# Backward log-softmax on one core: y in pieces of 5120 and 11264 columns, the first piece ahead of each store, and hand-made synchronization

## The chip, the cores and the metric

The kernel runs on one core of a Trainium2 chip. Times are device microseconds (us) of that core. A few words used below: VectorE (DVE in the profile), ScalarE (ACT) and SyncE (SP; its DMA issues are SPq) are engines of the core. A transfer is issued by SyncE into a queue that 16 DMA engines work off; every transfer here is split over all 16. A "packet" is one row of a transfer as the trace records it, with its start, duration and size. The profile's span runs from the first to the last instruction; a launch takes about 1.8 us more than its span (1867.19 against 1865.4 us in the profiled run of the kernel before).

## The reference

```python
# y, dy: (8, 1024, 8192) float32
def reference(y, dy):
    softmax_x = np.exp(y)
    sum_dy = np.sum(dy, axis=-1, keepdims=True)
    return dy - softmax_x * sum_dy
```

Each of 8192 rows is independent. The work is to read y and dy once and to write the result once: 805 MB.

## The kernel before

The rows go through in 32 groups of 256: 128 partitions with R = 2 rows each, so a group is 128 x 16384 numbers (8.4 MB) of each array. dy is loaded whole and the result overwrites it. y comes in two loads of 8192 columns. There are two buffers for dy and one for each half of y. The Tile framework places all waits.

```python
    R = 2
    CD = D // 2
    # dyp: 2 buffers of [P, R * D]; yp: R buffers of [P, D]          (cut)

    def load_dy(g):
        dy_t = dyp.tile([P, R * D], fp32, name="dy_t")
        nc.sync.dma_start(out=dy_t[:], in_=dy_v[g])
        s_t = stats.tile([P, R], fp32, name="s_t")
        nc.vector.tensor_reduce(out=s_t[:], in_=..., op=ALU.add, negate=True)   # (cut)
        return dy_t, s_t

    def load_y(g):
        y_ts = []
        for r in range(R):
            y_t = yp.tile([P, D], fp32, name="y_t")
            nc.sync.dma_start(out=y_t[:], in_=y_v[g][:, r * D : (r + 1) * D])
            y_ts.append(y_t)
        return y_ts

    def compute(dy_t, s_t, y_ts):
        for r in range(R):
            for c in range(0, D, CD):
                e = y_ts[r][:, c : c + CD]
                d = dy_t[:, r * D + c : r * D + c + CD]
                nc.scalar.activation(e, e, EXP)
                nc.vector.scalar_tensor_tensor(
                    out=d, in0=e, scalar=s_t[:, r : r + 1], in1=d, op0=ALU.mult, op1=ALU.add
                )
    # ...
    cur = load_dy(0)
    for g in range(G):
        if g < G - 1:
            y_ts = load_y(g)
            compute(*cur, y_ts)
            nxt = load_dy(g + 1)
            if g < G - 2:
                store(g, cur[0])
                cur = nxt
            # ... (the last store is cut in two)
```

In steady state SyncE issues: store of group g, both y loads of g+1, and, when that store has landed, dy of g+2.

## Time and profile before

| | kernel before |
|---|---|
| time, median of the 6 runs taken with those of the changed kernel | 1867.28 us |
| span of the profiled run | 1865.4 us |
| VectorE / ScalarE busy | 60% / 25% |
| DMA queue q1, share of 16 engines | 99.9% |
| rate over the span | 432 GB/s |

The first view is the page of the kernel before. The digits are busy tenths in 40 equal slices of the span; part 3 gives the time of the packets as a share of 16 engines; part 4 is the chain of waits, followed back from the last instruction; in part 5 the numbers after the bar are busy us, mean ns of one, and idle us before it with what ended it.

```profile
span 1865.4 us, 712 instructions
DVE 1119.2 (60%) x160; ACT 457.1 (25%) x129; POOL 0.2 (0%) x4
...
DMA  9999999999999999999999999999999999999999
...
q1 hardware_dynamic: 18576, 805.31, 99.9%
HBM read 536.87 MB, written 268.44 MB: 432 GB/s over the span
...
DMA y_t<-in_y_dram 69%; DVE dy_t L70 15%; ACT y_t L69 6%; DMA dy_t<-in_dy_dram 3%; DVE s_t L47 2%; DMA out_dram<-dy_t 1%; SPq L60 1%; SPq L77 1%; DVEq L122 0%; ACTq L69 0%; DVEq L70 0%
...
L69 ACT ACTIVATE y_t<-y_t 128x4096 f32<-128x4096 f32 x128 | 455.9, 3608 | 1375.6 <-DMA y_t<-in_y_dram 1375.6
```

Two readings of this page compete. By the chain, nearly one us in four is VectorE or ScalarE work (15 + 6 + 2%), so less of it, or earlier, should help. By the DMA row, the transfers never stop, and the engines' work lies behind them. The timeline decides how near the queue comes to running dry. Here are SyncE's issues in two late groups (start us, duration, instruction, count), and the VectorE sum that starts when dy is seen to have landed.

```profile
1709.76 0.33 SPq L45 DMA_DIRECT2D dy_t<-in_dy_dram  x1
...
1741.77 0.34 SPq L77 DMA_DIRECT2D out_dram<-dy_t  x1
1742.21 0.85 SPq L60 DMA_DIRECT2D y_t<-in_y_dram  x2
1748.49 17.22 DVE L47 TENSOR_REDUCE s_t<-dy_t 128x2 f32<-128x16384 f32 x1 [6.75 <-DMA dy_t<-in_dy_dram]
1767.83 0.33 SPq L45 DMA_DIRECT2D dy_t<-in_dy_dram  x1
```

The store is issued at 1741.77, and dy, the last transfer ahead of it in the queue, is seen to have landed at 1748.49. I call these 6.7 us the lead of the store. As long as the lead is large enough, the 16 engines pass from one transfer to the next without a stop. The dy load of 1767.83 has two y loads ahead of it.

### The profile page before, as it was taken

What the parts mean: (1) busy time and instruction counts of PE and PEld (TensorE: products, weight loads), DVE (VectorE), ACT (ScalarE), POOL (GpSimd) and SP (SyncE); (2) the same over time, 40 slices, a digit from 0 to 9 for tenths busy, and PEclk for the clock granted to TensorE, in tenths of its full rate; (3) what the DMA queues carried; (4) which work ended last, traced back from release to release, by engine and by line L of the source; (5) the groups of instructions that cost most, each with busy time, mean ns of one, the idle gap of its engine ahead of it and who ended that gap; (6) DMA issues with size and microseconds to landing.
All of it is one profiled execution on the core that took longest, in us unless ns stands there. A gap on an engine that the chain in (4) does not pass through costs nothing.

```text
span 1865.4 us, 712 instructions
## 1 busy us (share of the span) xinstructions
DVE 1119.2 (60%) x160; ACT 457.1 (25%) x129; POOL 0.2 (0%) x4
## 2 busy tenths in 40 slices
DVE  5675555755557555575555755657656576565664
ACT  2123321233212332123321233212332113331132
POOL 0000000000000000000000000000000000000000
DMA  9999999999999999999999999999999999999999
GB/s 427 416 434 431 443 433 422 435 437 436 427 433 431 440 430 434 431 429 441 433 437 425 433 442 431 434 425 436 438 434 433 428 434 437 437 431 430 429 435 396
DMA packets 18582, 805.36 MB, mean 432 GB/s; under 512 B 2064, under 2 KB 2064, under 8 KB 2064
## 3 DMA queue, kind: packets, MB, share of 16 engines
q1 hardware_dynamic: 18576, 805.31, 99.9%
q14 instruction: 6, 0.05, 0.0%
HBM read 536.87 MB, written 268.44 MB: 432 GB/s over the span
## 4 chain that ended last, share of the span: by engine, by line
DMA 74%; DVE 17%; ACT 6%; SPq 1%; issue 1%; DVEq 0%; ACTq 0%
DMA y_t<-in_y_dram 69%; DVE dy_t L70 15%; ACT y_t L69 6%; DMA dy_t<-in_dy_dram 3%; DVE s_t L47 2%; DMA out_dram<-dy_t 1%; SPq L60 1%; SPq L77 1%; DVEq L122 0%; ACTq L69 0%; DVEq L70 0%
## 5 line engine op out<-in xcount | busy, mean ns | idle before, releaser
L70 DVE SCALAR_TENSOR_TENSOR dy_t<-y_t,s_t,dy_t 128x4096 f32<-128x4096 f32 x128 | 568.1, 4481 | 490.3 <-ACT y_t L69 490.1
L69 ACT ACTIVATE y_t<-y_t 128x4096 f32<-128x4096 f32 x128 | 455.9, 3608 | 1375.6 <-DMA y_t<-in_y_dram 1375.6
L47 DVE TENSOR_REDUCE s_t<-dy_t 128x2 f32<-128x16384 f32 x32 | 551.0, 17220 | 232.1 <-DMA dy_t<-in_dy_dram 232.1
L69 ACT ACT_TABLE_LOAD x1 | 1.3, 1283 | 0.7 <-PEq L111 0.7
L111 POOL MEMSET const-bfloat16-1.0<- 128x1 bf16 x1 | 0.1, 102 | 0.0
L111 POOL MEMSET const-uint8-127<- 128x1 uint8 x1 | 0.1, 102 | 0.0
L111 POOL MEMSET const-float32-1.0<- 128x1 f32 x1 | 0.1, 99 | 0.0
L111 POOL MEMSET const-float32-0.0<- 128x1 f32 x1 | 0.1, 98 | 0.2 <-issue 0.2
## 6 DMA issues: line engine op xcount, KB each, us to landing
y_t<-in_y_dram SPq DMA_DIRECT2D x64, 4096.0 KB, 35.9
out_dram<-dy_t SPq DMA_DIRECT2D x2, 4096.0 KB, 22.6
dy_t<-in_dy_dram SPq DMA_DIRECT2D x32, 38.7
out_dram<-dy_t SPq DMA_DIRECT2D x31, 26.1
```

The lines of the kernel that those rows point to most:

```text
L47: nc.vector.tensor_reduce(out=s_t[:], in_=dy_t[:].rearrange("p (r d) -> p r d", r=R), axis=mybir.AxisListType.X, op=ALU.add, negate=True,)
L60: nc.sync.dma_start(out=y_t[:], in_=y_v[g][:, r * D : (r + 1) * D])
L69: nc.scalar.activation(e, e, EXP)
L70: nc.vector.scalar_tensor_tensor(out=d, in0=e, scalar=s_t[:, r : r + 1], in1=d, op0=ALU.mult, op1=ALU.add)
L77: nc.sync.dma_start(out=out_v[g][:, k * w : (k + 1) * w], in_=dy_t[:, k * w : (k + 1) * w])
L111: nc = _bacc.Bacc("TRN2", target_bir_lowering=False, num_devices=1)
```

## The change

Its intent is to make the lead larger and better balanced. y of a group is cut into 5120 and 11264 columns. The first piece needs only a part of the buffer that the group before has done with early, so it can be queued ahead of the store, after dy. While VectorE finishes the group, dy and that piece keep the queue filled. The dy load that waits for the store to land has the second piece, 11264 columns, ahead of it. The work on the second piece is cut so that its first multiply-add starts early (1024, 2048, 2048, 3072, 3072 columns). All engines are synchronized by hand in one critical section, with every wait written out, and the first dy load is cut in two.

```diff
+    A = 5120
+    PIECES = [(0, A), (A, 6144), (6144, 8192), (8192, 10240), (10240, 13312), (13312, W)]   # lines joined
+    x_ts = [pool.tile([P, W], fp32, name=f"x{j}") for j in range(2)]
+    y_t = pool.tile([P, W], fp32, name="y_t")
+    with tc.tile_critical(no_gpsimd_drain=True):
+        # ... semaphores, one per purpose
+        def load_ya(g):
+            if g:
+                nc.sync.wait_ge(dve_done, K * (g - 1) + 1)
+            nc.sync.dma_start(out=y_t[:, :A], in_=y_v[g][:, :A]).then_inc(ya_in, 16)
+        def load_yb(g):
+            if g:
+                nc.sync.wait_ge(dve_done, K * g)
+            nc.sync.dma_start(out=y_t[:, A:], in_=y_v[g][:, A:]).then_inc(yb_in, 16)
+        # ... first dy in two halves, load_ya(0)
+        for g in range(G - 1):
+            load_yb(g)
+            if g >= 1:
+                nc.sync.wait_ge(out_done[(g + 1) % 2], 16 * ((g + 1) // 2))
+            j = (g + 1) % 2
+            nc.sync.dma_start(out=x_ts[j][:], in_=dy_v[g + 1]).then_inc(dy_in[j], 16)
+            load_ya(g + 1)
+            if g == G - 2:
+                load_yb(g + 1)
+            else:
+                nc.sync.wait_ge(dve_done, K * (g + 1))
+            nc.sync.dma_start(out=out_v[g], in_=x_ts[g % 2][:]).then_inc(out_done[g % 2], 16)
+        # ... last store in two halves, waits for all stores; loops of ScalarE and VectorE over PIECES
-    cur = load_dy(0)
-    for g in range(G):
-        if g < G - 1:
-            y_ts = load_y(g)
-            compute(*cur, y_ts)
-            nxt = load_dy(g + 1)
-            if g < G - 2:
-                store(g, cur[0])
-        # ...
```

More of the change, by code (lines that the diff above doesn't have):

```diff
@@ L30 @@
     R = 2
+    W = R * D
     G = N // (P * R)
-    assert N == G * P * R
-    CD = D // 2
+    assert N == G * P * R and D == 8192 and G >= 3
+    A = 5120
+    PIECES = [
+        (0, A),
+        (A, 6144),
+        (6144, 8192),
+        (8192, 10240),
+        (10240, 13312),
+        (13312, W),
+    ]
+    K = len(PIECES)
+    ROW0 = 3
     y_v = y.flatten_outer_dims().rearrange("(g p r) d -> g p (r d)", p=P, r=R)
@@ L37 @@
     out_v = out.flatten_outer_dims().rearrange("(g p r) d -> g p (r d)", p=P, r=R)
-    dyp = ctx.enter_context(tc.tile_pool(name="dyp", bufs=2))
-    yp = ctx.enter_context(tc.tile_pool(name="yp", bufs=R))
-    stats = ctx.enter_context(tc.tile_pool(name="stats", bufs=2))
-    def load_dy(g):
-        dy_t = dyp.tile([P, R * D], fp32, name="dy_t")
-        nc.sync.dma_start(out=dy_t[:], in_=dy_v[g])
-        s_t = stats.tile([P, R], fp32, name="s_t")
-        nc.vector.tensor_reduce(
-            out=s_t[:],
-            in_=dy_t[:].rearrange("p (r d) -> p r d", r=R),
-            axis=mybir.AxisListType.X,
-            op=ALU.add,
-            negate=True,
-        )
-        return dy_t, s_t
@@ L56, in load_y @@
-    def load_y(g):
-        y_ts = []
-        for r in range(R):
-            y_t = yp.tile([P, D], fp32, name="y_t")
-            nc.sync.dma_start(out=y_t[:], in_=y_v[g][:, r * D : (r + 1) * D])
-            y_ts.append(y_t)
-        return y_ts
-    def compute(dy_t, s_t, y_ts):
-        for r in range(R):
-            for c in range(0, D, CD):
-                e = y_ts[r][:, c : c + CD]
-                d = dy_t[:, r * D + c : r * D + c + CD]
-                nc.scalar.activation(e, e, EXP)
-                nc.vector.scalar_tensor_tensor(
-                    out=d, in0=e, scalar=s_t[:, r : r + 1], in1=d, op0=ALU.mult, op1=ALU.add
-                )
@@ L74, in store @@
-    def store(g, dy_t, parts=1):
-        w = R * D // parts
-        for k in range(parts):
-            nc.sync.dma_start(
-                out=out_v[g][:, k * w : (k + 1) * w], in_=dy_t[:, k * w : (k + 1) * w]
-            )
-    cur = load_dy(0)
-    for g in range(G):
-        if g < G - 1:
-            y_ts = load_y(g)
-            compute(*cur, y_ts)
-            nxt = load_dy(g + 1)
-            if g < G - 2:
-                store(g, cur[0])
-                cur = nxt
-            else:
-                held, cur = cur, nxt
-        else:
-            y_ts = load_y(g)
-            compute(*cur, y_ts)
-            store(g - 1, held[0])
-            store(g, cur[0], parts=R)
+    pool = ctx.enter_context(tc.tile_pool(name="pool", bufs=1))
@@ new lines @@
+    x_ts = [pool.tile([P, W], fp32, name=f"x{j}") for j in range(2)]
+    y_t = pool.tile([P, W], fp32, name="y_t")
+    s_ts = [pool.tile([P, R], fp32, name=f"s{j}") for j in range(2)]
+    with tc.tile_critical(no_gpsimd_drain=True):
+        dy_in = [nc.alloc_semaphore(f"dy_in{j}") for j in range(2)]
+        dy_in_row = nc.alloc_semaphore("dy_in_row")
+        ya_in = nc.alloc_semaphore("ya_in")
+        yb_in = nc.alloc_semaphore("yb_in")
+        out_done = [nc.alloc_semaphore(f"out_done{j}") for j in range(2)]
+        row_done = nc.alloc_semaphore("row_done")
+        exp_done = nc.alloc_semaphore("exp_done")
+        sum_done = nc.alloc_semaphore("sum_done")
+        dve_done = nc.alloc_semaphore("dve_done")
+        def load_ya(g):
[6 more added lines that the diff above has]
+            nc.sync.dma_start(out=y_t[:, A:], in_=y_v[g][:, A:]).then_inc(yb_in, 16)
+        nc.sync.dma_start(out=x_ts[0][:, :D], in_=dy_v[0][:, :D]).then_inc(dy_in_row, 16)
+        nc.sync.dma_start(out=x_ts[0][:, D:], in_=dy_v[0][:, D:]).then_inc(dy_in[0], 16)
+        load_ya(0)
+        for g in range(G - 1):
[10 more added lines that the diff above has]
+            nc.sync.dma_start(out=out_v[g], in_=x_ts[g % 2][:]).then_inc(out_done[g % 2], 16)
+        last = x_ts[(G - 1) % 2]
+        nc.sync.wait_ge(dve_done, K * (G - 1) + ROW0)
+        nc.sync.dma_start(out=out_v[G - 1][:, :D], in_=last[:, :D]).then_inc(row_done, 16)
+        nc.sync.wait_ge(dve_done, K * G)
+        nc.sync.dma_start(out=out_v[G - 1][:, D:], in_=last[:, D:]).then_inc(
+            out_done[(G - 1) % 2], 16
+        )
+        nc.sync.wait_ge(out_done[(G - 2) % 2], 16 * (G // 2))
+        nc.sync.wait_ge(row_done, 16)
+        nc.sync.wait_ge(out_done[(G - 1) % 2], 16 * (G // 2))
+        for g in range(G):
+            for k, (b, e) in enumerate(PIECES):
+                if k == 0:
+                    nc.scalar.wait_ge(ya_in, 16 * (g + 1))
+                elif k == 1:
+                    nc.scalar.wait_ge(yb_in, 16 * (g + 1))
+                nc.scalar.activation(y_t[:, b:e], y_t[:, b:e], EXP).then_inc(exp_done, 1)
+        for g in range(G):
+            x, s = x_ts[g % 2], s_ts[g % 2]
+            for c, w, sem, v in (
+                [(0, D, dy_in_row, 16), (D, D, dy_in[0], 16)]
+                if g == 0
+                else [(0, W, dy_in[g % 2], 16 * (g // 2 + 1))]
+            ):
+                nc.vector.wait_ge(sem, v)
+                nc.vector.tensor_reduce(
+                    out=s[:, c // D : (c + w) // D],
+                    in_=x[:, c : c + w].rearrange("p (r d) -> p r d", d=D),
+                    axis=mybir.AxisListType.X,
+                    op=ALU.add,
+                    negate=True,
+                ).then_inc(sum_done, 1)
+            nc.vector.wait_ge(sum_done, g + 2)
+            for k, (b, e) in enumerate(PIECES):
+                r = b // D
+                nc.vector.wait_ge(exp_done, K * g + k + 1)
+                nc.vector.scalar_tensor_tensor(
+                    out=x[:, b:e],
+                    in0=y_t[:, b:e],
+                    scalar=s[:, r : r + 1],
+                    in1=x[:, b:e],
+                    op0=ALU.mult,
+                    op1=ALU.add,
+                ).then_inc(dve_done, 1)
```

## The prediction

> **What bounds the kernel now.** The transfers, and nothing else. The page's DMA row is 9 in all 40 slices, queue q1 is busy 99.9% of the 16 engines' span, and 805.31 MB move at a mean of 432 GB/s. VectorE is busy 60% and ScalarE 25%. In the DMA records of the trace the typical 64 KB packet takes 2.418 us and the typical 32 KB packet 1.213 us, which is 433.7 and 432.2 GB/s over 16 engines. The Trainium skill ("DMA: Bandwidth & Descriptors", section "Where 436 GB/s comes from") puts the ceiling of the fabric at 435.2 GB/s; this trace agrees, it runs 0.4% under it while packets flow. Engine by engine I find six gaps of 0.3 us in the whole run.
>
> The chain of waits looks different: 69% of it is the wait for y, 15% VectorE, 6% ScalarE. I read that as a queue that is always full: a y load takes 44.5 us from issue to landing although its 4 MB need about 9.7 us, so it stands behind other transfers. The steady period of a group is 58.08 us (chain view, 1452.30 to 1510.38), and one group's packets per engine are 16 x 2.418 + 16 x 1.213 = 58.1 us. So the period holds no bubble.
>
> **Why the queue never empties before.** In the timeline a store is issued at 1741.77; the load of dy ahead of it is seen landed at 1748.49, so the store is 6.7 us early. The next dy load is issued at 1767.83, when the store has landed, with the two y loads (19.4 us of packets) still queued.
>
> **What the change does.** The bytes are the same. The issues go from 129 to 130, with pieces of 20 and 44 KB a partition instead of twice 32 KB. From the two packet times a packet costs about 8 ns plus 0.0368 ns per byte (estimate), so 20 + 44 KB cost 2.43 us, as 2 x 1.213 do: nothing. The queue order becomes dy(g+1), first y piece, store(g), rest of y. Estimates from 4096-column durations (ScalarE 3.56 us, VectorE 4.44 us): after the rest of y lands, the five pieces end about 14 us later, while dy plus the first piece keep the queue filled for 25 us, so the store is some 11 us early instead of 7. The next dy load waits for the store with 13.3 us of y behind it: again 11 us spare. A margin over zero buys no time. Splitting the first dy is off the path too. Hand-made waits add short instructions, inside slack.
>
> **What lies on the critical path.** The head (first packet 1.7 us after the start), the packets (about 1859 us), and the tail (last packet to end 1.2 us). Packets that run over their typical time sum to about 4 us an engine. Only head, tail and this excess can move, by a microsecond or so.
>
> **Predicted:** 1867.4 us, 8 in 10 between 1865.6 and 1869.4. Chances: faster by over 2% 0.01, within 2% 0.98, slower 0.01.
>
> **Right if** the DMA row stays at 9, q1 at about 99.9%, the rate at 432 GB/s, the period at 58.1 us; the waits of the engines and the chain's labels change much; and the store's issue leads the landing of the transfers ahead of it by about 11 us.
>
> **Wrong if** 20 KB packets or the new order of reads and writes run at another rate (period not 58.1 us at full queue: the packet times would show it), if some wait holds SyncE longer than the queued work lasts (DMA slices under 9), or if the hand synchronization adds microseconds at the start or end of the kernel (first packet later than 1.7 us, last packet to end over 1.2 us).

## The result

| | before | changed |
|---|---|---|
| median of 6 runs, us | 1867.28 | 1869.47 |
| lowest to highest, us | 1866.88 to 1867.93 | 1868.34 to 1869.74 |
| span of the profiled run, us | 1865.4 | 1867.7 |

The ratio is 1.001, with a 95% interval of 0.9997 to 1.0023: the same at the 2% mark. The changed kernel is 2 us slower, 0.1%, and in these runs the two ranges don't overlap.

The page of the changed kernel, the lines that answer to those shown of before:

```profile
span 1867.7 us, 633 instructions
DVE 1130.5 (61%) x225; ACT 463.3 (25%) x193; POOL 0.2 (0%) x4
...
DMA  9999999999999999999999999999999999999998
...
q1 hardware_dynamic: 18720, 805.31, 99.8%
HBM read 536.87 MB, written 268.44 MB: 431 GB/s over the span
...
DMA y_t<-in_y_dram 70%; DVE x L136 19%; ACT y_t L114 5%; DMA x<-in_dy_dram 2%; DMA out_dram<-x 2%; DVE s L125 1%; SPq L95 1%; SPq L73 0%; SPq L82 0%; SPq L81 0%; SPq L169 0%; SPq L58 0%
...
L114 ACT ACTIVATE y_t<-y_t 128x5120 f32<-128x5120 f32 (+2 forms) x192 | 462.0, 2469 | 1373.6 <-DMA y_t<-in_y_dram 1373.6
```

ScalarE's wait for y is as long as it was (1373.6 against 1375.6 us), and the queue is as full. Its timeline at the same place:

```profile
1745.14 0.34 SPq L95 DMA_DIRECT2D out_dram<-x  x1
1745.53 0.43 SPq L78 DMA_DIRECT2D y_t<-in_y_dram  x1
1750.30 17.22 DVE L125 TENSOR_REDUCE s<-x 128x2 f32<-128x16384 f32 x1 [5.19 <-DMA x<-in_dy_dram]
1756.38 4.47 ACT L114 ACTIVATE y_t<-y_t 128x5120 f32<-128x5120 f32 x1 [15.46 <-DMA y_t<-in_y_dram]
1767.56 5.55 DVE L136 SCALAR_TENSOR_TENSOR x<-y_t,s,x 128x5120 f32<-128x5120 f32 x1
1775.72 0.33 SPq L89 DMA_DIRECT2D x<-in_dy_dram  x1
...
1789.01 9.97 ACT L114 ACTIVATE y_t<-y_t 128x1024 f32<-128x1024 f32 x5 [28.16 <-DMA y_t<-in_y_dram]
```

The store goes out at 1745.14, and the transfer ahead of it is now the first piece of y, which lands at 1756.38: a lead of 11.2 us in place of 6.7. The dy load of 1775.72 leads the landing of the second piece at 1789.01 by 13.3 us, where that of the kernel before (1767.83) led the landing of the second y load (1787.27) by 19.4. So 6.7 and 19.4 us have become 11.2 and 13.3, larger where it was small and better balanced. The intent was met. The steady group shows what it brought. The view is of one group's period, its length, busy us of VectorE, ScalarE and GpSimd, clock, DMA share and GB/s, first in the kernel before.

```profile
1452.30:1510.38 58.08, 34.98 (x5) 14.25 (x4) 0.00 (x0) 1.00 1.00 433
```

The same view of the changed kernel:

```profile
1455.25:1513.31 58.06, 35.33 (x7) 14.44 (x6) 0.00 (x0) 1.00 1.00 433
```

The period is the time that the packets need, in both, at 433 GB/s.

To place the 2 us, I cut each span into the head (up to the first packet of data), the stretch of packets, and the tail (after the last packet), from the packet records:

```
                 span     head   packets  tail
before          1865.42   1.74   1862.46  1.22
before_again    1864.71   1.73   1861.76  1.21
before_hand     1866.08   1.94   1862.47  1.67
after           1867.65   1.96   1864.05  1.64
after_again     1866.79   1.95   1863.20  1.64
after_even      1867.03   1.96   1863.41  1.66
```

(The runs other than "before" and "after" are described below.) The head is 0.2 us and the tail 0.4 us longer in the changed kernel. The other 1.6 us arise between the packets of the first ten groups: the last sum of the steady part starts 1.8 us later than before, and it did so 1.9 us later by the tenth group already.

### The profile page after: what moved, and what is told of

The parts are those of the page before. It is cut to its first block, busy times and chain, and to the rows that moved or that the text cites. A ratio compares the mean times of both kernels' runs of the same rounds, so it can differ in the third digit from the quotient of the medians. Undisturbed runs are those within 1.5% of the kernel's fastest.

```text
span 1867.7 us, 633 instructions
## 1 busy us (share of the span) xinstructions
DVE 1130.5 (61%) x225; ACT 463.3 (25%) x193; POOL 0.2 (0%) x4
## 4 chain that ended last, share of the span: by engine, by line
DMA 73%; DVE 20%; ACT 5%; SPq 1%; issue 0%
DMA y_t<-in_y_dram 70%; DVE x L136 19%; ACT y_t L114 5%; DMA x<-in_dy_dram 2%; DMA out_dram<-x 2%; DVE s L125 1%; SPq L95 1%; SPq L73 0%; SPq L82 0%; SPq L81 0%; SPq L169 0%; SPq L58 0%
## 5 line engine op out<-in xcount | busy, mean ns | idle before, releaser
L136 DVE SCALAR_TENSOR_TENSOR x<-y_t,s,x 128x5120 f32<-128x5120 f32 (+2 forms) x192 | 579.3, 3059 | 538.3 <-ACT y_t L114 537.2
L114 ACT ACTIVATE y_t<-y_t 128x5120 f32<-128x5120 f32 (+2 forms) x192 | 462.0, 2469 | 1373.6 <-DMA y_t<-in_y_dram 1373.6
L125 DVE TENSOR_REDUCE s<-x 128x2 f32<-128x16384 f32 (+1 forms) x33 | 551.2, 16703 | 174.8 <-DMA x<-in_dy_dram 174.8
```

Of the source, the lines that this page charges most:

```text
L114: nc.scalar.activation(y_t[:, b:e], y_t[:, b:e], EXP).then_inc(exp_done, 1)
L125: nc.vector.tensor_reduce(out=s[:, c // D : (c + w) // D], in_=x[:, c : c + w].rearrange("p (r d) -> p r d", d=D), axis=mybir.AxisListType ...
L136: nc.vector.scalar_tensor_tensor(out=x[:, b:e], in0=y_t[:, b:e], scalar=s[:, r : r + 1], in1=x[:, b:e], op0=ALU.mult, op1=ALU.add,).then_i ...
```

## The experiments

The theory: the queue of transfers is the bound, in both kernels, and a lead beyond what keeps it full buys nothing. The rivals: the chain is right that the engines' work is part of the path; or something was gained in the steady part and lost elsewhere.

### 1. Nearly no compute: after_tiny

```diff
-nc.scalar.activation(y_t[:, b:e], y_t[:, b:e], EXP)
+nc.scalar.activation(y_t[:, b:b + 64], y_t[:, b:b + 64], EXP)
 # likewise 64 columns in each sum and in each multiply-add
```

> The changed kernel with every exp, sum and multiply-add cut to 64 columns of its piece; all transfers and waits stay (the result is wrong on purpose). Theory (the transfers are the bound, the engines only wait for them): 1867 to 1870 us, no faster than the kernel before, within 0.2% of it; VectorE and ScalarE under 3% busy. Rival (the chain of waits is right that VectorE and ScalarE make up 20 to 25% of the path): 1400 to 1500 us.

Measured: 1869.64 us (4 runs), ratio 1.0009. The page of this run:

```profile
span 1867.0 us, 633 instructions
DVE 52.6 (3%) x225; ACT 36.3 (2%) x193; POOL 0.2 (0%) x4
...
DMA  9999999999999999999999999999999999999998
...
q1 hardware_dynamic: 18720, 805.31, 99.9%
```

VectorE's work fell from 1130.5 to 52.6 us, and the time did not move. The quarter of the chain that was put down to VectorE and ScalarE was not worth one us. The chain is true as a story of who released whom, but each y load that it counts had stood in a full queue, and a y load that is issued later stands there for a shorter time.

A remark on the side: the comparison with the reference let this kernel pass, although it computes a wrong result. A softmax over 8192 columns averages 1/8192. If dy is drawn with a spread of 1, a sum of 8192 draws has a size of about 90, so the term is about 0.01 beside a dy of about 1. Here a passed comparison is weak evidence that a kernel is right.

### 2. The same added work in both kernels: plus4, plus9, plus17

If the lead is what the change altered, it must show when each group gets more work ahead of its store. The added work is a sum over columns of y that nothing uses, before the last multiply-add; the result stays right.

```diff
# kernel before, in compute(), after the activation
+                if r == R - 1 and c == D - CD:
+                    j_t = junk.tile([P, 1], fp32, name="j_t")
+                    nc.vector.tensor_reduce(out=j_t[:], in_=y_ts[r][:], axis=..., op=ALU.add)
# changed kernel, VectorE loop, after the wait for the exp
+                if k == K - 1:
+                    nc.vector.tensor_reduce(out=junk[:, g : g + 1], in_=y_t[:, A : A + D], axis=..., op=ALU.add)
# plus4: 4096 of the columns; plus17: the sum of 8192 twice
```

> The kernel before with one added sum of 8192 columns of y (about 8.6 us on VectorE) in each group, ahead of the last multiply-add, so each store is issued some 8.6 us later. Theory (the store leads the end of the dy packets by some 5 us, so 8.6 us overrun the lead by about 3 us in each of 31 groups): 1950 us, 1920 to 1980, the DMA queue no longer full (q1 about 95%). Rival (VectorE has 40% idle time, so 8.6 us of it cost nothing): 1867 us.

> The changed kernel with the same added sum of 8192 columns (about 8.6 us) ahead of the last multiply-add of each group. Theory (the first piece of y ahead of the store makes the lead about 10 us, more than 8.6): 1869 to 1873 us, q1 still over 99.5%. Rival (both kernels have the same slack): the same loss as the kernel before with the same added work, some 80 us.

> The kernel before with one added sum of 4096 columns (about 4.4 us) in each group, so a store is issued only some 2.3 us before the landing of dy is seen, as it was 2.6 us before the landing of the first piece of y in the changed kernel with 8.7 us added. Theory (what counts is the lead of the store, whatever the kernel): a loss of the same kind, about 0.8 us a group, 1885 to 1905 us in all. Rival (the changed kernel's loss with 8.7 us added was its own, from its pieces or waits): 1867 us.

> The changed kernel with the same 4.4 us added in each group; its store should still lead by some 6.9 us, as that of the kernel before does with nothing added. Theory: 1868 to 1870 us, no loss against the changed kernel. Rival: the loss of before_plus4.

> The kernel before with two added sums of 8192 columns (17.3 us in a group). With 8.68 us added it lost 4.38 us a group, so once the lead is used up every added us should be a us of the period: 58.07 + 4.38 + 8.6 = 71.0 us a group, 2260 to 2280 us.

> The changed kernel with the same 17.3 us added. Its store's lead was 11.2 us against 6.75 us, so it should lose 4.5 us a group less than the kernel before with the same work: 66.6 us a group, 2120 to 2145 us. If the lead is no longer what counts, 71 us as the other.

| added per group (trace) | kernel before | changed kernel |
|---|---|---|
| nothing | 1867.28 us | 1869.47 us |
| 4.41 us (plus4) | 1892.00, ratio 1.0122 (1.0107 to 1.0137) | 1869.57, ratio 1.0005 (0.9989 to 1.0022) |
| 8.68 us (plus9) | 2000.26, ratio 1.0709 (1.0693 to 1.0725) | 1882.55, ratio 1.0071 (1.0054 to 1.0089) |
| 17.27 us (plus17) | 1981.30 (2 runs; not the same order, see below) | 2137.39 (2 runs) |

All ratios are against the unaltered kernel before. With 4.41 us added, the kernel before loses 1.2% and the changed one nothing; with 8.68 us it is 7.1% against 0.7%. This is what the change is worth, and it is not a matter of time saved. The expectations held for the plus4 runs and for after_plus17. after_plus9 missed its 1869 to 1873 us (four runs, 1878.19 to 1892.74): a lead of 2.6 us was not enough, as section 3 shows. One of the four runs of after_plus4, the profiled one, took 1875.92 us, the others 1869.21 to 1869.62. Its trace is of that long run, and it matters: the store leads by 7.1 us (1521.03 to 1528.10),

```profile
1521.03 0.34 SPq L96 DMA_DIRECT2D out_dram<-x  x1
...
1528.10 4.47 ACT L115 ACTIVATE y_t<-y_t 128x5120 f32<-128x5120 f32 x1 [15.62 <-DMA y_t<-in_y_dram]
```

more than in the kernel before, and yet its late groups take 58.1 to 58.7 us and don't settle.

The timeline of before_plus9 shows the store issued when dy had already landed: the sum over dy started right behind the last multiply-add, without a wait.

```profile
1499.08 4.47 DVE L77 SCALAR_TENSOR_TENSOR dy_t<-y_t,s_t,dy_t 128x4096 f32<-128x4096 f32 x1
1503.47 17.21 DVE L48 TENSOR_REDUCE s_t<-dy_t 128x2 f32<-128x16384 f32 x1
1503.58 0.34 SPq L84 DMA_DIRECT2D out_dram<-dy_t  x1
```

The 16 engines stood idle between packets for 107 us each on average in that run, and their packets overran their typical time by 30 us, where they do so by some 4 us in the kernel before. The two together, less those 4 us, are the 133 us by which its span is longer. I had expected a loss of 3 us a group, 1920 to 1980 us in all, and got 4.4 (a period of 62.45 us, 2000.26 in all): about 3.5 us of it are idle time (107 us over 31 groups), and about 0.8 the longer packets, of which I had not thought.

The second part stands alone in after_plus9, and in before_plus4, where the engines were never idle for more than a few us in all. The view is of one group's period in after_plus9.

```profile
1480.15:1539.04 58.89, 43.83 (x9) 14.43 (x6) 0.00 (x0) 1.00 1.00 427
```

The DMA share is 1.00, and yet the rate is 427 GB/s and not 433. Nothing is idle; packets have become longer. In the packet records of that group the excess lies where the engines pass from the store to the next load: the last 64 KB packets of the store take 2.64 to 3.34 us in place of 2.42.

after_plus17 was predicted from before_plus9 alone, by adding work and subtracting the difference of the leads, as 66.6 us a group; its trace has 66.56.

before_plus17 fell far outside: 1981 us where 2260 to 2280 were expected, faster than before_plus9 with half of the added work. The timeline of SyncE tells why. First before_plus9, whose order is that of the kernel before:

```profile
1503.58 0.34 SPq L84 DMA_DIRECT2D out_dram<-dy_t  x1
1504.02 1.34 SPq L61 DMA_DIRECT2D y_t<-in_y_dram  x2
1525.38 0.33 SPq L46 DMA_DIRECT2D dy_t<-in_dy_dram  x1
```

And the same view of before_plus17:

```profile
1508.01 0.33 SPq L46 DMA_DIRECT2D dy_t<-in_dy_dram  x1
1512.38 0.33 SPq L61 DMA_DIRECT2D y_t<-in_y_dram  x1
1547.58 0.34 SPq L84 DMA_DIRECT2D out_dram<-dy_t  x1
1548.01 0.38 SPq L61 DMA_DIRECT2D y_t<-in_y_dram  x1
```

I had added work, and the framework had answered by placing the first y load of the next group ahead of the store, which is the very idea of the change. The run says nothing about the kernel before with 17 us added. It does say that the order alone, with the framework's waits and pieces of 8192, carries 17.27 us of added work at 61.3 us a group. That is 5.3 us a group better than the changed kernel with the same work (66.56), so the cut at 5120 is not what bears the work: a first piece of 8192 columns bears more (after_even, in section 4, has such a piece, and its store leads by 17.6 us).

### 3. Which part of the change gives the lead: after_old_order

```diff
             nc.sync.dma_start(out=x_ts[j][:], in_=dy_v[g + 1]).then_inc(dy_in[j], 16)
-            load_ya(g + 1)
             # wait for the group, store
             nc.sync.dma_start(out=out_v[g], in_=x_ts[g % 2][:]).then_inc(out_done[g % 2], 16)
+            load_ya(g + 1)
 # (for the last two groups it stays as it was)
```

> The changed kernel with the first piece of y behind the store again, as in the kernel before. If the 2 us come from the order of the transfers: 1867.3 to 1867.9 us. If not: 1869 us. The store should then lead the landing of dy by some 5 us, enough to keep the queue full: steady group 58.07 us.

Measured: 1874.67 us (1872.91 to 1874.69, 5 runs), ratio 1.0025, and 6 us over after_again, the changed kernel in the same rounds. Neither expectation was right. The store has the lead that I had worked out, here 5.3 us:

```profile
1516.08 0.34 SPq L95 DMA_DIRECT2D out_dram<-x  x1
...
1521.35 17.22 DVE L127 TENSOR_REDUCE s<-x 128x2 f32<-128x16384 f32 x1 [5.31 <-DMA x<-in_dy_dram]
```

but that is not quite enough: the groups take between 58.08 and 59.03 us to the end, and never settle at 58.07. So cutting y at 5120 without moving the piece ahead makes the kernel worse, since the larger second piece takes longer to work through. The order is what gives the lead.

The leads of the traced runs, side by side. The lead is the time from the issue of the store to the landing of the transfer ahead of it, late in each run (the last 15 groups of the steady part). Such a landing is seen when the last of the 16 engines is done; the next column gives the time from the issue of the store to the first of these 16 landings. The period is taken from the starts of the sums over dy. A negative lead says that the store was issued after the landing.

| run | lead, us | to the first landing, us | group period, us |
|---|---|---|---|
| after_tiny | 24.0 | 20.3 to 20.7 | 58.05, once 58.4 |
| after_even (section 4) | 17.6 | 14.2 to 14.4 | 58.07 |
| changed kernel | 11.2 | 6.9 to 7.0 | 58.07 |
| after_plus4 (the long run) | 6.9 to 7.3 | 1.7 to 2.4 | 58.1 to 58.7 |
| before_hand (section 4) | 6.8 | 3.6 to 3.8 | 58.07 |
| kernel before | 6.7 | 3.3 to 3.5 | 58.07 |
| after_old_order | 5.1 to 6.0 | 1.1 to 2.4 | 58.1 to 59.0 |
| after_plus9 | 2.6 to 2.9 | 1.1 to 1.9 | 58.5 to 59.3 |
| before_plus4 | 2.4 to 2.5 | 0.5 to 1.8 | 58.2 to 59.7 |
| before_plus17 | -0.8 | -1.3 | 61.3 |
| before_plus9 | -1.9 | -2.4 | 62.45 |
| after_plus17 | -6.0 | -6.3 | 66.56 |

Leads of 6.7, 11.2, 17.6 and 24.0 us all give the same period: more than enough buys nothing. Below zero the period grows by a us for each us of lead that is missing, in three programs with different orders, pieces and waits. In between, the lead alone does not tell which run loses: 6.7 us are enough in the kernel before, and up to 7.3 are not in the traced run of after_plus4. The time to the first landing does tell: every run with 3.3 us or more holds 58.07, every run with 2.4 us or less loses. It fits that the engine that is done first is the one that runs short of work; in after_old_order and after_plus4 the first landings, after two groups at the start, keep the pace of 58.07 us until the engines have drifted so far apart that less than 3 us are left. This is read from the traces; no run has set this time by itself.

With before_plus4 and after_plus9, two kernels with different orders, pieces and waits lose something at nearly the same lead, which rules out the rival named in the expectation of before_plus4 (no loss there). The sizes are not equal: the ratios are 1.0122 and 1.0071, and their intervals don't overlap.

A small lead may also show in the scatter. The 31 runs of the kernel before reach from 1866.74 to 1873.53 us, six of them over 1869.8; the 11 of the changed kernel lie within 1868.22 and 1869.74. In the rounds that they shared last, the kernel before reached 1873.28 and after_again 1869.16. No such long run of the kernel before was traced, so it is not shown that the lead is the reason.

### 4. Where the 2 us come from: after_even, before_again, after_again, before_hand

```diff
# after_even: y in two pieces of 8192 columns, six pieces of work as before
-    A = 5120
+    A = 8192
# before_again, after_again: the two kernels once more, without an edit
# before_hand: the old order, pieces (4 x 4096) and whole first dy, written with the hand-made waits
```

> The changed kernel with y in two pieces of 8192 columns, so all packets are 32 or 64 KB as before. If the 20 and 44 KB packets cost the 2 us by which the changed kernel is slower, this one takes 1867.3 us; if the cost is in the hand synchronization, in the order, or is the chance of how the 16 engines fall into step in the first groups, 1868.5 to 1870 us. In either case the steady group takes 58.07 us.

> The kernel before, once more under its own name, to see how far two programs that are the same come out apart, and whether its trace again takes some six groups until the group period falls to 58.07 us. If the 2 us between the two kernels are real: 1866.9 to 1868 us, ratio 1.000 within 0.0005. If they are chance: as far from the kernel before as the changed one was (2 us).

> The changed kernel once more. If the 2 us are real: 1868.3 to 1869.8 us again, with a start some 0.2 us and an end some 0.4 us longer than in the kernel before and the rest in the first ten groups. If they are chance: nearer 1867.3 us.

> The kernel before (its pieces, its order of transfers, the first dy whole) written with the hand synchronization of the changed one. If the 2 us come from the hand synchronization: 1868.5 to 1869.5 us, or about 0.6 us over the kernel before if only the start and the end are longer (1867.9 us). If they come from the order or the piece sizes: 1867.3 us.

Measured: after_even 1869.08 us (1868.81 to 1869.31), before_again 1867.02 (1866.49 to 1869.35), after_again 1868.66 (1868.22 to 1869.16), before_hand 1868.10 (1867.69 to 1873.49). The kernel before itself gave 1866.74 to 1873.28 us in the rounds of the last three, a median of 1869.53 of 11 runs, so by times alone these runs don't tell 2 us apart: the ratio of before_again is 0.9989 and of after_again 0.9996, and both intervals hold 1. The parts of the spans, in the table above, are steadier.

- The hand-made synchronization costs 0.6 us: all kernels that have it show a head of 1.94 to 1.97 us in place of 1.74, and a tail of 1.6 to 1.7 in place of 1.2. before_hand has nothing but this; its packets take 1862.47 us, as before. SyncE issues the first load at 0.95 us in the changed kernel and at 0.73 in the kernel before.
- The 20 and 44 KB packets cost nothing that I can see. Their typical times are 0.762 and 1.665 us, together 2.427, against 2.426 for two of 32 KB, and after_even, with none of them, has the packets' stretch of the changed kernel (1863.41 against 1863.20 and 1864.05 us).
- The rest, some 1.3 us (a mean of 1863.6 against 1862.2 us for the three runs of the old order with a full lead), arises in the first groups, in which all these kernels are slower than 58.07 us.

For the last point I worked out from the landing records how far apart the 16 engines finish one dy load (the last minus the first of the 16), beside the time to the next dy load:

```
group           1     2     3     4     5     6     7     8     9    10
before  spread 0.63  0.97  1.00  1.35  1.72  1.96  2.74  2.74  2.88  2.90
        period 58.50 58.12 58.43 58.41 58.28 58.88 58.05 58.19 58.07 58.16
after   spread 0.40  0.43  0.61  0.66  0.79  1.21  1.87  3.06  3.62  3.79
        period 58.81 58.22 58.15 58.20 58.79 58.73 59.22 58.61 58.23 58.06
```

The engines start in step and drift apart until their landings spread over 3 or 4 us, and from then on the period of these two kernels is 58.07 us. The two rows of a kernel are not independent: the period runs from last landing to last landing, so a widening spread is itself part of it. In the kernel before, these ten periods exceed 58.07 us by 2.4 us in all, and from group 1 to group 11 the spread widens by 2.4 us, while the first of the 16 landings keeps the pace of 58.07 us all along. In the changed kernel the excess is 4.3 us, and 3.4 of it are the widening. So most of this loss is that some engines fall behind the first one and don't catch up; why they do is open.

One could think that engines in step are slow because all pass from a load to a store at the same time. In before_plus4 and after_plus9, where the store comes late, the spread does stay between 0.4 and 2 us to the end, and the first and the last landing lose alike (23 and 25 us over 30 groups). But in after_old_order and after_plus4 the late groups lose at spreads of 3 to 5 us, and in the changed kernel groups 2 to 4, with spreads of 0.4 to 0.7 us, lose less than groups 5 to 8 with 0.8 to 3.1. The traces don't bear this reading out, and no run has set the spread by itself.

The number of groups until 58.07 us is not a mark of the kernel: it is six in the kernel before and eight in before_again, which is the same program, nine in the changed kernel and six in after_even. What the order, the halves of the first dy and the smaller pieces of work each add to the 1.3 us is open too. A run of the changed kernel with the first dy whole would tell a part of it; it was not made.

I did not find a version that beats both. By the kernel before's own records, the data packets of one engine at their typical times (504 of 64 KB at 2.418 us and 528 of 32 KB at 1.213) make 1859 us, an estimate from the trace; only the settling, the head and the tail are left, a few us of 1867.

## Why the prediction was right

- "The transfers, and nothing else": right, and shown by after_tiny, which takes away 95% of VectorE's work for no gain.
- The ceiling of 435.2 GB/s, which the Trainium skill ("DMA: Bandwidth & Descriptors", section "Where 436 GB/s comes from") gives for the 16 ports, was one ground for expecting no gain: the steady groups of both kernels run at 433 GB/s, and no run has a steady period under 57.9 us. The same section says that between HBM and SBUF the HBM side, at about 358 GB/s a core, is what binds. The prediction left that out; the 433 GB/s of this one core don't agree with it.
- The period of 58.1 us and the lead of 11 us: as written (58.06 and 11.2). The second margin was put at 11 us and is 13.3 from issue to landing.
- "The waits of the engines and the chain's labels change much": this did not happen. The wait for y is 70% of the chain after 69%, ScalarE 5% after 6, VectorE 20% after 17, and ScalarE's wait for y is 1373.6 us after 1375.6.
- "Hand-made waits add short instructions, inside slack": not quite. They lengthen the head and the tail, which have no slack: the first packet comes at 1.96 us and the tail is 1.64, over the 1.7 and 1.2 that the prediction named under "wrong if". It is 0.6 us in all, not microseconds, but it is over a quarter of the difference.
- "A margin over zero buys no time": right in that the step from 6.7 to 11.2 us bought none. Wrong about zero: at 5.1 to 6.0 us groups already lose, in one run even at 6.9 to 7.3, and at 2.4 to 2.6 us a group loses about 0.8 us. The kernel before was nearer to its edge than I had read.
- The size: 1867.4 us predicted, 1869.47 measured. The median is just over the end of the range, 1869.4, and the mean of the six runs, 1869.25, just inside; that it came so near is in part luck, for the 2 us were not foreseen. They lie in the head (0.2), the tail (0.4) and the stretch of packets (1.6), terms that the prediction had let move "by a microsecond or so". The excess that it named for the packets did not grow: it is 4.0 us an engine before and 4.1 after. The stretch ends with the slowest engine, and a part of the 1.6 is that this one falls further behind the first (4.3 us at the last dy landing after 3.5); the rest is not resolved.

## What to carry to other kernels

When a queue of transfers is full and its rate is at its ceiling, the waits that a chain shows behind it are not gains to be had: shrink the work in question to almost nothing once, and see. A change of order that makes the issue of a store earlier buys tolerance, not time, where the lead was already large enough; measure what it is worth by adding the same work to both kernels. Count a lead to the first of the engines that is done and not only to the landing that a semaphore shows: here that told which runs lose. And look at the rate beside the share of busy time, for a queue can be 100% busy with packets that have become longer.

## What the Trainium skill lacked or had wrong

- "DMA: Bandwidth & Descriptors", "Measured (HBM→SBUF, 128 partitions, SWDGE, issued from GpSimd)", lists 425 GB/s for a large transfer on a lone core. With loads and stores mixed two to one, the settled groups here run at 433 GB/s, so nearer to the 435.2 of the same page. Against its statement that the HBM side binds at about 358 GB/s between HBM and SBUF (section "Where 436 GB/s comes from"), one core moves 433 here.
- The same page gives a fixed cost of about 2 us for one transfer on the path from GpSimd (section "Anatomy of one DMA — SWDGE (gpsimd) path"; here SyncE issues), but no page says how early a transfer has to be issued behind a full queue to be free: here it was free where the first of the 16 engines had 3.3 us or more of work left, not quite with 2.4 or less, and a lead of 2.4 to 2.6 us to the last landing cost about 0.8 us in 58.
- That the 16 engines finish independently stands on that page ("Why a DMA increments its semaphore by 16 and not by 1"), and agrees. That they drift apart over several groups, from a spread of 0.65 us to some 3 us, and that a group measured by its last landing is slower meanwhile (25.17 MB in 58.5 us are 430 GB/s, in 59.2 us 425, in 58.07 us 433), is on no page.
- "Perfetto Trace Analysis", section "Identifying the Most-Contended Engine", says that occupancy misleads for DMA and to use HBM utilization, so a rate, instead. after_plus9 agrees and gives a number: a share of 1.00 at 427 GB/s against 1.00 at 433.
